# Sums of squares for the norms: additions on VectorE in place of products with ones on TensorE

## The chip, the cores and the metric

One core of one Trainium2 chip runs the whole program in one launch. The metric is the device time of that core in microseconds; the time before is the median of 3 runs. The engines are named as in the profile: PE (TensorE), DVE (VectorE), ACT (ScalarE), POOL (GpSimd), SP (SyncE, which here only issues transfers).

## The reference, cut to what matters

A transformer trunk of two layers works on 256 context tokens and 1024 latent tokens, 1280 in all, with 1024 features in f32. Each layer normalises its tokens, projects them, runs four mixers (mLSTM, latent attention, SSD, S5), projects back, normalises again and runs a feed-forward part of width 2816. The change concerns one function, which occurs with 1024, 256 and 128 features:

```python
def rmsnorm(x, g):
    x32 = x.astype(jnp.float32)
    y = x32 * lax.rsqrt(jnp.mean(x32 * x32, axis=-1, keepdims=True) + EPS)
    return (y * g.astype(jnp.float32)).astype(x.dtype)
```

It is called for both norms of each layer (with a modulation by shift and scale), for the output norm of the SSD mixer, and for the compressed queries, keys and values of the attention. A last norm follows the second layer. (In the kernel, one mixer's per-head norm is computed elsewhere and is not touched.)

## The kernel before, in words

Activations are feature-major: a tile has 128 features on the partitions and tokens along the row. 1024 features are eight tiles. Tokens come in groups of 256 (the context), 512 and 512; layer 1 leaves the context out after its mixers.

A dense product (`dense_acc`, lines 242 to 244) is three matmuls per tile of 128 features, since every f32 operand is split into a leading and a remaining part (`split`, lines 202 and 203). It runs through two PSUM banks, or through five where `many()` is on (the output projection, the feed-forward part, the first products of layer 1).

`rstd` (lines 173 to 197) makes 1/sqrt(mean of squares) for up to 512 tokens, and puts it on every partition. Per tile, ACT squares it (line 181) into a buffer of two, and PE multiplies the squares by a column block of 32 ones (line 183). Tiles go in turn to the four groups of 32 columns of PE's array, so that up to four partial sums lie on four groups of 32 partitions in one PSUM bank. ACT then copies the bank to the tile `sb` (line 186). For each 128 tokens one narrow product (line 188) has 128 columns of `sb` as its stationary operand and a selector column `msel`, with a one on one partition of each group of 32, as its moving operand: it adds up the four partial sums and turns the tokens onto the partitions. DVE scales and adds EPS (line 190), POOL takes the power -0.5 (line 192), PE transposes the broadcast result back (line 194), ACT copies it to SBUF (line 196).

`rstd` is called 30 times:

- at the start, for the three groups (lines 1456 to 1470), eight tiles each; the tile for `sb` has one buffer there, and the squares go to another pool's four buffers;
- in `latent_norms` (line 794), one tile (keys and values) or two (queries) per group, both layers;
- in the SSD outputs (line 650), two tiles per group, both layers, with one buffer that `sb` and the broadcast share;
- in `norm_mod` (line 218) for the second norm of each layer (lines 1623 and 1625), eight tiles per group; `norm_apply` then takes two DVE operations and one ACT operation per tile (lines 212, 214, 215);
- in `done` (lines 1634 to 1646), after the last feed-forward products of a group: in layer 0 the next layer's first norm, in layer 1 the final norm, whose result DVE multiplies in (line 1644) and ACT's queue sends out.

Around the norms of `done` and of lines 1623 and 1625, each dense product of a tile is followed by the residual on DVE, which reads the PSUM bank and updates x (line 1601). x is what line 181 squares.

The order in which the engines work is not that of the text. The program is built with `schedule_with_timeline_sim=True` (line 1829): the builder places the instructions of all engines by a timeline that it simulates, and each engine then takes its own queue in that order. Weight loads on SP's queue are issued within `ahead()`.

## Time and profile before

| what | value |
|---|---|
| median of 3 runs | 3555.32 us (3553.36 to 3558.95) |
| span of the profiled execution, first to last instruction | 3550.2 us |
| mean granted TensorE clock of that execution | 0.981 |
| PE busy, matmuls | 3418.2 us |
| PEld busy, weight loads | 2795.2 us |
| DVE busy | 1708.2 us |
| ACT busy | 1106.9 us |
| POOL busy | 889.9 us |
| products with ones, line 183 | 138 matmuls, 276 records |

The profiled execution's own time is its span, 3550.2 us, and what little lies outside of the first and last instruction; the runs' times are taken without a profile. A matmul of two f32 operands shows as two records. A matmul's start is measured, its end is modelled, and matmuls overlap: distances from start to start tell what one costs in a stream. "idle" in a row is the time in which the engine did nothing just before, with what released it. [...]

### The profile page before, as it was taken

To read this page: it belongs to the slowest core of one execution; us is meant where nothing else is said; L and a number is where in the kernel's file an instruction comes from. 1 tells how busy PE (TensorE), PEld (TensorE's weight loads), DVE (VectorE), ACT (ScalarE), POOL (GpSimd) and SP (SyncE) were. 2 spreads that over 40 slices of the span, in tenths; PEclk is the share of its full clock that TensorE was granted. 3 is DMA by queue.
4 is the path that set the end of the run, shared out by engine and by line. 5 is a ranking of instruction groups with operands and counts; after the bars stand their busy time and mean duration, and the time that the engine had idled before them with its cause. 6 is when DMAs were issued, how large, how long until landed. Compare 5 with 4: busy or idle time off the path is not lost. (4 is left out here: it accounts for less than half of the span.)

```text
span 3550.2 us, 48986 instructions
## 1 busy us (share of the span) xinstructions
PE 3418.2 (96%) x19154; PEld 2795.2 (79%) x19186; DVE 1708.2 (48%) x3597; ACT 1106.9 (31%) x1885; POOL 889.9 (25%) x1061
## 2 busy tenths in 40 slices
PE   8899998999999999999999999998999999999998
PEld 6888995676768888888887889985666688888885
DVE  6857727554365486333323563636633432232333
ACT  4224534334242211111223324533333312212222
POOL 1922424011033222222221011331110223323321
PEclk9899998999999999999999999998999999999999
DMA  5577533345111121111112655542153111111111
GB/s 200 166 205 229 156 119 113 110 140 212 65 46 62 54 90 72 36 36 36 42 40 81 162 166 164 142 150 67 60 204 107 42 42 54 53 42 54 48 46 62
DMA packets 264904, 352.84 MB, mean 99 GB/s; under 512 B 89240, under 2 KB 190304, under 8 KB 264672
## 3 DMA queue, kind: packets, MB, share of 16 engines
q1 hardware_dynamic: 168148, 265.90, 23.5%
q10 hardware_dynamic: 96524, 83.81, 7.5%
q8 instruction: 151, 2.47, 0.3%
q14 instruction: 81, 0.66, 0.1%
HBM read 266.09 MB, written 83.52 MB: 98 GB/s over the span
## 5 line engine op out<-in xcount | busy, mean ns | idle before, releaser
L1601 DVE SCALAR_TENSOR_TENSOR x<-pd,modv,x 128x512 f32<-128x512 f32 (+1 forms) x448 | 299.8, 687 | 233.6 <-PE pd L244 233.2
L242 PE MATMUL pd<-fh,wh_d 128*128 128x512 f32 (+1 forms) x896 | 325.3, 369 | 9.3 <-ACT fh L202 5.7
L242 PE MATMUL ps_g<-hb,wh_g 128*128 128x512 f32 (+1 forms) x880 | 326.0, 370 | 3.2 <-ACT hb L214 2.2
L244 PE MATMUL ps_g<-hb,wl_g 128*128 128x512 f32 (+1 forms) x880 | 324.4, 369 | 2.5 <-POOL wl_g L203 2.5
L243 PE MATMUL pd<-fl,wh_d 128*128 128x512 f32 (+1 forms) x896 | 326.0, 367 | 0.7 <-POOL fl L203 0.7
L244 PE MATMUL pd<-fh,wl_d 128*128 128x512 f32 (+1 forms) x896 | 325.5, 368 | 0.0
L242 PE MATMUL ps_u<-hb,wh_u 128*128 128x512 f32 (+1 forms) x880 | 325.4, 370 | 0.0
L243 PE MATMUL ps_g<-hb,wh_g 128*128 128x512 f32 (+1 forms) x880 | 325.1, 369 | 0.0
L243 PE MATMUL ps_u<-hb,wh_u 128*128 128x512 f32 (+1 forms) x880 | 324.7, 369 | 0.0
L244 PE MATMUL ps_u<-hb,wl_u 128*128 128x512 f32 (+1 forms) x880 | 324.3, 369 | 0.2 <-POOL wl_u L203 0.2
L662 DVE SCALAR_TENSOR_TENSOR cv<-gp,vec,cv 128x1281 f32<-128x1281 f32 (+1 forms) x44 | 72.6, 1651 | 476.8 <-ACT cv L659 476.8
L242 PE MATMUL ps_in<-ha,wh_in 128*128 128x384 f32 (+3 forms) x688 | 218.3, 326 | 13.5 <-ACT st L1426 13.5
L203 POOL TENSOR_TENSOR wl_u<-wr_u,wh_u 128x1024 fp32r<-128x1024 f32 x44 | 105.5, 2397 | 481.7 <-ACT wh_u L202 481.7
L243 PE MATMUL ps_in<-ha,wh_in 128*128 128x384 f32 (+3 forms) x688 | 222.4, 323 | 0.0
L244 PE MATMUL ps_in<-ha,wl_in 128*128 128x384 f32 (+3 forms) x688 | 221.2, 322 | 0.0
L242 PE MATMUL ps_in<-hb,wh_in 128*128 128x256 f32 (+1 forms) x704 | 212.7, 305 | 0.8 <-ACT hb L214 0.6
L244 PE MATMUL ps_in<-hb,wl_in 128*128 128x256 f32 (+1 forms) x704 | 212.8, 303 | 0.0
L243 PE MATMUL ps_in<-hb,wh_in 128*128 128x256 f32 (+1 forms) x704 | 212.5, 302 | 0.2 <-DVE hb L215 0.2
L242 PEld LDWEIGHTS pd<-fh,wh_d 128*128 128x128 f32 x896 | 169.1, 189 | 45.8 <-DVE x L1601 7.4
L202 ACT CAST wh_u<-wr_u 128x1024 fp32r<-128x1024 f32 x44 | 46.3, 1051 | 502.4 <-PE pd L243 436.5
L242 PEld LDWEIGHTS ps_g<-hb,wh_g 128*128 128x128 f32 x880 | 166.2, 189 | 36.4 <-ACT hb L214 3.5
L243 PEld LDWEIGHTS pd<-fl,wh_d 128*128 128x128 f32 x896 | 169.4, 189 | 31.9 <-issue 1.7
(509 smaller groups left out, 7691.2 us busy)
## 6 DMA issues: line engine op xcount, KB each, us to landing
wm<-in_w_mod SPq DMA_DIRECT2D x96, 512.0 KB
wr_in<-in_w_in SPq DMA_DIRECT2D x44, 512.0 KB
wr_g<-in_w_up SPq DMA_DIRECT2D x44, 512.0 KB
wr_u<-in_w_up SPq DMA_DIRECT2D x44, 512.0 KB
wr_d<-in_w_down SPq DMA_DIRECT2D x44, 512.0 KB
wr_out<-in_w_out SPq DMA_DIRECT2D x32, 512.0 KB
PF<-st ACTq DMA_DIRECT2D x100, 128.0 KB
PF<-st ACTq DMA_DIRECT2D x60, 192.0 KB
```

What stands on the lines that cost most here:

```text
L202: nc.scalar.copy(hi, src)
L203: (eng or nc.gpsimd).tensor_tensor(lo, src, hi.bitcast(F32), OP.subtract)
L242: nc.tensor.matmul(ps, whi(k), ahi(k), start=start and i == 0, stop=False)
L243: nc.tensor.matmul(ps, whi(k), alo(k), start=False, stop=False)
L244: nc.tensor.matmul(ps, wlo(k), ahi(k), start=False, stop=stop and i == len(ks) - 1)
L662: nc.vector.scalar_tensor_tensor(dst, src[:, 0:n], w0, dst, OP.mult, OP.add)
L1601: nc.vector.scalar_tensor_tensor(v, ps, K.modv[l][:, 8 * part + m, c:c + 1], v, OP.mult, OP.add)
```

## The change

In `rstd`, ACT squares the first tile straight into `sb`. Each further tile is squared into its buffer as before, and DVE adds it to `sb`. The products with 32 columns of ones and the copy of the bank to `sb` are gone. The PSUM bank is taken after that; the narrow product for each 128 tokens has a column of ones as its moving operand, over all 128 partitions. What follows is as before.

```diff
     def rstd(self, tiles, nfeat, n, pool, name, bufs=2, out=None, sqs=None):
         nc = self.nc
         ntc = n // P
-        ng = min(len(tiles), 4)
-        ps = self.psm.tile([P, 512], F32, tag="m", name=f"ss_{name}")
+
+        sb = pool.tile([P, 512], F32, tag="rb", name=f"sb_{name}", bufs=bufs)
         for i, x in enumerate(tiles):
+            if not i:
+                nc.scalar.activation(sb[:, :n], x, AF.Square)
+                continue
             sq = sqs(f"sq_{name}_{i}") if sqs else pool.tile([P, 512], F32, tag="sq", name=f"sq_{name}_{i}", bufs=bufs)
             nc.scalar.activation(sq[:, :n], x, AF.Square)
-            g = i % 4
-            nc.tensor.matmul(ps[32 * g:32 * g + 32, :n], self.ones[:, :32], sq[:, :n], start=i < 4, stop=i >= len(tiles) - ng)
-        sb = pool.tile([P, 512], F32, tag="rb", name=f"sb_{name}", bufs=bufs)
-        r_ = slice(0, 32 * ng)
-        nc.scalar.copy(sb[r_, :n], ps[r_, :n])
+            nc.vector.tensor_tensor(sb[:, :n], sb[:, :n], sq[:, :n], OP.add)
+        ps = self.psm.tile([P, 512], F32, tag="m", name=f"ss_{name}")
         for j in range(ntc):
-            nc.tensor.matmul(ps[:, j:j + 1], sb[r_, j * P:j * P + P], self.msel[r_, 0:1], start=True, stop=True)
+            nc.tensor.matmul(ps[:, j:j + 1], sb[:, j * P:j * P + P], self.ones[:, 0:1], start=True, stop=True)
         v = pool.tile([P, 8], F32, tag="rs", name=f"rv_{name}", bufs=4)
```

The rest of the diff takes comments out and leaves their lines empty.

## Rows read from the trace of the kernel before

**Rows 1.** The page's first part: busy time (share of the span) xinstructions, by engine.
```profile
PE 3418.2 (96%) x19154; PEld 2795.2 (79%) x19186; DVE 1708.2 (48%) x3597; ACT 1106.9 (31%) x1885; POOL 889.9 (25%) x1061
```

**Rows 2.** Line 183 by stretches: us, PE busy, PEld busy, clock, DMA share, GB/s.
```profile
0.00:40.00 40.00, 11.22 (x48) 3.14 (x48) 0.91 0.88 308
190.00:300.00 110.00, 8.13 (x18) 1.24 (x18) 1.00 0.82 234
400.00:510.00 110.00, 5.42 (x12) 0.82 (x12) 1.00 0.33 95
920.00:1005.00 85.00, 18.19 (x48) 2.64 (x48) 1.00 0.14 47
1905.00:1962.00 57.00, 19.35 (x48) 3.34 (x48) 0.97 0.33 116
2100.00:2160.00 60.00, 6.89 (x14) 0.96 (x14) 1.00 0.44 146
2270.00:2340.00 70.00, 4.18 (x8) 0.55 (x8) 1.00 0.33 95
2690.00:2795.00 105.00, 12.04 (x32) 1.68 (x32) 0.99 0.28 101
3500.00:3540.00 40.00, 15.66 (x48) 3.06 (x48) 0.99 0.11 40
sum 677.00, PE 101.10 PEld 17.43; mean PE 11.23 PEld 1.94
```

**Rows 3.** All instructions by stretches: us, PE, PEld, DVE, ACT, POOL busy, clock, DMA.
```profile
0.00:40.00 40.00, 25.97 (x234) 14.59 (x235) 11.65 (x42) 21.00 (x40) 14.22 (x11) 0.91 0.88 308
190.00:300.00 110.00, 103.77 (x661) 92.83 (x662) 73.22 (x201) 28.74 (x62) 22.07 (x47) 1.00 0.82 234
...
920.00:1005.00 85.00, 85.00 (x363) 55.48 (x363) 29.07 (x48) 29.16 (x50) 9.76 (x9) 1.00 0.14 47
```

**Rows 4.** PE in order of time: start us, us, what; around products of line 183.
```profile
986.97 1.05 PE L183 MATMUL ss_n<-sq_n,ones 128*32 128x512 f32 x4
...
1931.85 0.62 PE L183 MATMUL ss_n<-sq_n,ones 128*32 128x256 f32 x2
...
3502.28 0.39 PE L243 MATMUL pd<-fl,wh_d 128*128 128x512 f32 x1
3502.51 0.40 PE L244 MATMUL pd<-fh,wl_d 128*128 128x512 f32 x1
3502.83 1.04 PE L183 MATMUL ss_fin<-sq_fin,ones 128*32 128x512 f32 x2
3503.81 0.50 PE L242 MATMUL pd<-fh,wh_d 128*128 128x512 f32 x1
```

**Rows 5.** DVE lines: duration ns min/median/max; the last one by form, mean ns.
```profile
L764 DVE TENSOR_TENSOR m_u<-m_u,m_r x18: 681/691/693, 608.2 to 2571.8; 128x512 f32<-128x512 f32 x18
L1154 DVE TENSOR_TENSOR zm_V<-zm_pis,zm_y x32: 408/417/539, 85.6 to 1230.1; 128x256 f32<-128x256 f32 x32
L1601 DVE SCALAR_TENSOR_TENSOR x<-pd,modv,x 128x512 f32<-128x512 f32 x344 | 253.6, 749 | 211.5 <-PE pd L244 211.3
```

**Rows 6.** Three more stretches, columns as in rows 3.
```profile
1908.00:1984.00 76.00, 71.82 (x338) 47.97 (x337) 48.84 (x79) 33.15 (x60) 5.31 (x6) 0.98 0.26 92
2790.00:2800.00 10.00, 5.64 (x23) 2.75 (x20) 2.10 (x4) 3.59 (x6) 1.01 (x1) 0.77 0.01 2
2800.00:2810.00 10.00, 10.00 (x34) 7.79 (x34) 9.12 (x14) 4.27 (x7) 0.00 (x0) 0.72 0.00 0
```

**Rows 7.** PE in order of time, at the start: idle before, and what ended it.
```profile
28.75 0.64 PE L151 MATMUL pm<-wm,sc 128*32 128x128 f32 x16 [2.39 <-DMA wm<-in_w_mod]
```

**Rows 8.** Groups of 3490 to 3550: busy us, mean ns, idle before and releasers.
```profile
L1601 DVE SCALAR_TENSOR_TENSOR x<-pd,modv,x 128x256 f32<-128x256 f32 (+1 forms) x24 | 13.5, 572 | 18.9 <-PE pd L244 18.9
L1644 DVE SCALAR_TENSOR_TENSOR x<-x,vec,rbs_fin 128x256 f32<-128x256 f32 (+1 forms) x24 | 11.9, 569 | 6.4 <-ACT rbs_fin L196 6.4
```

**Rows 9.** Line 181, the squares: duration ns min/median/max, first and last start, forms.
```profile
L181 ACT ACTIVATE sq_n<-x x64: 402/630/636, 878.3 to 2791.3; 128x512 f32<-128x512 f32 x48, 128x256 f32<-128x256 f32 x16
```

## The prediction, made before the change was built

> **What bounds the kernel now.** The page's first part comes first: PE is busy for 96% of the span, DVE for 48% [rows 1]. An average does not say whether PE time that is taken out comes back, so the next view is the products of line 183 alone, stage by stage [rows 2]. They hold PE for 101.1 us, 2.8% of the span, in nine stretches: the start, the latent norms and the SSD norms of both layers, the second norm of both layers (920 and 2690), the norm for layer 1 (1905) and the final norm. Then all engines in those stretches [rows 3]: from 920 to 1005 PE is busy for all of 85 us, in the first 40 us for only 26.0. Line 183 has 138 matmuls and 276 records, two to a matmul.

> What one costs is read from starts, since the ends are modelled [rows 4]. Between dense products of 512 columns the starts are 0.23 us apart. With one 512-column product of line 183 between, they go from 3502.51 to 3503.81, 1.30 us: it costs 1.30 - 0.23 = 1.07 us, close to its record of 1.04. So the busy sums of rows 2 serve as the price. [...]

> **The change part by part.** Durations are those of the profiled execution: its span is 3550.2 us, 5.1 us less than the median of the runs, 3555.3, part of which lies outside the span. I take gains from the span and subtract them from the median.

> *Removed:* the 138 products, 101.1 us of PE, and 30 copies on ACT (line 186), which I cost at nothing in themselves: ACT is not the bound.

> *Added:* one addition per tile but the first. The 14 calls with eight tiles make 7 each, the 10 calls with two tiles one each: 98 + 10 = 108, of which 71 have 512 columns and 37 have 256. The nearest rows are additions or products of two f32 SBUF tiles on DVE: 0.69 us for 512 columns (0.68 to 0.69) and 0.42 for 256 (0.41 to 0.54) [rows 5]. Sum: 71 x 0.691 + 37 x 0.417 = 64.5 us on an engine that has 1842 us free; the dearest 256 would add 4.5.

> *Kept:* the narrow products per 128 tokens, as many as before, with ones in place of the selector. In the small calls they sum over 128 rows instead of 32 or 64; I take no difference, as the output has the same one column.

> *Moved:* the tile sb is taken before the first square, where it was taken after the last product. With two buffers, a group's first square now waits for the narrow products of the group before; at the start and in SSD, with one, for those products or for the last use of the broadcast. Nothing but squares of the same norm is queued behind that on ACT for long, and PE has dense work meanwhile; nothing. The PSUM bank is taken later and held for less; nothing, perhaps a gain. No DMA is added or moved by hand.

> By stages, with the PE time of rows 2:

> - Start, 11.2 us: **0**. PE waits there for the modulation weights, 2.39 us at 28.75 [rows 7], and DVE is idle for 28 of the 40 us [rows 3], enough cover for the 21 additions: 7 x 0.417 + 14 x 0.691 = 12.6 us. If they came late, up to 3 us are lost; without PE work until the weights land, the clock could stay low a little longer: -5 to 0 for both.
> - Latent norms, layer 0, 8.1: **4**, half. PE is busy for 104 of 110 us, but DVE works 73 on the scans beside it, and a chain there may set the end (0 to 8).
> - SSD norms, layer 0, 5.4; latent and SSD norms, layer 1, 6.9 and 4.2: **16.5**, in full. Dense products fill PE there.
> - Second norm, layer 0, 18.2: **18**. PE never idles, and DVE is busy for 29 of 85 us [rows 3].
> - Norm for layer 1, 19.4: **13**. From 1908 to 1984 DVE works 48.8 of 76 us on residuals and on applying the norm [rows 6]; the additions make it 48.8 + 12.6 = 61.4. That leaves 14.6 at most, less about 1.5 of waiting for the first sums. DVE becomes the bound here.
> - Second norm, layer 1, 12.0: **17**. Its last group gets its norm late, since each pair of squares waits for a product in PE's queue. PE is then idle for 4.4 us in 2790 to 2800, and in 2800 to 2810 the granted clock is 0.72, that is, some 5.6 us at 1.2 GHz, which costs 2.8 [rows 6]. With squares and additions off PE's queue the norm is ready while PE still has the first group's products; I count 5 of these 7.2 us (12 to 19).
> - Final norm, 15.7: **9**. DVE waits 18.9 us there for residuals and 6.4 for the broadcast [rows 8]; the additions take 7 x 0.691 + 14 x 0.417 = 10.7. What is left of 25.3 is 14.6, less the wait for the very first residual, about 3, and 2 to 3 for the chain behind the last sum: squares, one narrow product, power, transpose, copy. After the change DVE is late next.

> Sum: 0 + 4 + 16.5 + 18 + 13 + 17 + 9 = 77.5. 3555.3 - 78 = **3477 us**.

> Not shown by the trace: the order of every queue is built anew from a simulated timeline, SP's loads included. What a bad order costs is bounded by the tail of layer 1's second norm, 7 us; four such stages could each gain or lose one, so -28 to +28. I take 0, since nothing says which.

> **The rivals.**

> *A. DVE takes over, and only plain slots come back.* The tails stay as they are and the two stages in which DVE binds give nothing: 16.5 + 18 + 12 + 4 = 50, less 3 at the start: 47, **3508 us**. For it: DVE would be busy for 61 of 76 us around 1908. Against it: DVE is off the path in the other stages.

> *B. The products ran beside each other, so they are cheaper than they look.* At 986.97 two of them (four records) take 1.05 us together, what one takes alone [rows 4]. If a round of up to four always cost 1.07 us at 512 columns and 0.62 at 256 (the record at 1931.85), the 38 rounds after the start would hold PE for 26 x 1.07 + 12 x 0.62 = 35 us, and 3555 - 35 = **3520 us** comes out. Against it: those are rounds that seldom meet. Squares come one or two at a time, and the union of their records is 101 us already.

> [...]

> *C. Slower: the queue of DVE becomes a chain.* DVE works in order. If each addition is queued right behind its residual, DVE stands until ACT has squared that tile, and the next residual, which frees the PSUM bank that PE wants, stands behind it. Then a tile of 512 takes 0.75 (residual) + 0.63 (square) [rows 5, 9] + 0.69 (addition) + some 0.25 of crossings = 2.3 us, where PE needs 6 x 0.23 = 1.37: +0.95. With such gaps the clock falls as it did after the idle time at 2790 [rows 6]; at 1.2 GHz the tile's six products take twice as long, 2.76 us: +1.39. For the 77 additions of the large norms after the start this is 107 us against the 78 gained: 3555 - 78 + 107 = **3584 us**. It decides from 78 / 77 = 1.0 us of stall per addition. Against it: five banks and residuals of other groups are in flight and can be put between, and in the second norms dense products of other groups stand beside the residuals.

> **How the numbers follow.** What a measurement of this kernel can tell from no change is about 0.2%, 7 us. Chances: the forecast 0.61 (its own range 3450 to 3500: start -5, tails +-15, latent 0 to 8, final and layer 1 norms down to half), A 0.19, B 0.08, C 0.08, gains and losses that cancel 0.04. The range reaches from 3450, all slots outside the start (90 us) with both tails and a lucky order, to 3520, which takes in A and just reaches B. Faster: 0.61 + 0.19 + 0.08 = 0.88; same 0.04; slower 0.08.

> **What the changed profile would show.** PE's busy time falls by some 95 us to about 3320, and DVE's rises by some 65 to 1773. No product has 32 columns from line 183. From 920 to 1005 the same dense products take 18 us less. Around 2790 to 2810 PE shows no gap and the clock stays at 1.0. At the end DVE's rows stand nearly back to back. It would be wrong if residuals (line 1601) of a stage are spaced by more than 1.4 us with PE waiting for DVE, if the granted clock falls in the norm stages, or if the 100% stretches gain less than rows 2 give, with new waits of PE for something that is not DVE.

## The result, and the profile after

The changed kernel takes **3489.7 us** (median of 4 runs, 3485.1 to 3493.4), the kernel before 3554.9 in the same comparison: a ratio of 0.9816, 95% interval 0.9803 to 0.983. That is 65 us faster where 78 were forecast, inside the range. The profiled executions say the same: the span goes from 3550.2 to 3483.2 us, 67.0 less.

Busy time by engine, the page's first part, of the changed kernel; it answers to [rows 1]:

```profile
PE 3316.9 (95%) x18910; PEld 2782.9 (80%) x18910; DVE 1758.5 (50%) x3705; ACT 1092.4 (31%) x1853; POOL 893.4 (26%) x1061
```

PE loses 101.3 us: all that line 183 held [rows 2]. DVE gains 50.3. The additions' own records, all of them line 185 in the changed kernel (duration ns min/median/max, first and last start in us, forms):

```profile
L185 DVE TENSOR_TENSOR sb_n<-sb_n,sq_n x77: 415/682/2667, 9.7 to 2727.3; 128x512 f32<-128x512 f32 x56, 128x256 f32<-128x256 f32 x21
L185 DVE TENSOR_TENSOR sb_fin<-sb_fin,sq_fin x21: 410/426/683, 3436.5 to 3472.1; 128x256 f32<-128x256 f32 x14, 128x512 f32<-128x512 f32 x7
L185 DVE TENSOR_TENSOR sb_ln<-sb_ln,sq_ln x5: 426/682/693, 248.1 to 2111.1; 128x512 f32<-128x512 f32 x4, 128x256 f32<-128x256 f32 x1
L185 DVE TENSOR_TENSOR sb_s_r<-sb_s_r,sq_s_r x5: 426/693/827, 413.9 to 2286.7; 128x512 f32<-128x512 f32 x4, 128x256 f32<-128x256 f32 x1
```

There are 108 (77 + 21 + 5 + 5), 71 of 512 columns and 37 of 256, at 0.68 and 0.42 us: as forecast from [rows 5].

All engines in four stretches that the prediction named (us, then busy time of PE, PEld, DVE, ACT, POOL, the granted clock, DMA); the first two answer to [rows 3], the others to the norm for layer 1 in [rows 6], which now comes some 25 to 35 us earlier:

```profile
0.00:40.00 40.00, 17.66 (x167) 13.33 (x168) 22.31 (x67) 17.96 (x34) 14.66 (x11) 0.88 0.88 306
920.00:1005.00 85.00, 80.05 (x379) 65.19 (x378) 53.13 (x91) 36.57 (x55) 18.09 (x14) 0.98 0.14 43
...
1910.00:1920.00 10.00, 2.50 (x12) 2.02 (x11) 9.18 (x18) 5.71 (x10) 0.00 (x0) 0.72 0.58 193
1920.00:1930.00 10.00, 5.56 (x18) 4.56 (x19) 7.08 (x11) 5.74 (x9) 1.01 (x1) 0.50 0.35 122
```

From 920 to 1005 PE had not idled at all; now it idles for 5 us. In the norm for layer 1 it stands for 11.9 of 20 us while DVE is busy for 16.3, and the granted clock falls to 0.5, at which products of 384 columns start 0.32 us apart, not 0.17 as at 1.0 (0.98 over the whole stretch before, [rows 6]). PE's longest wait there, 7.5 us, is that of a narrow product (line 188) for the last addition of its group (line 185). The end of layer 1's second norm looks as forecast; it stood at 2790 to 2810 in [rows 6]:

```profile
2730.00:2740.00 10.00, 7.73 (x38) 6.01 (x38) 3.12 (x6) 3.08 (x5) 3.37 (x2) 1.00 0.16 52
2740.00:2750.00 10.00, 10.00 (x43) 7.66 (x43) 8.09 (x12) 4.32 (x7) 0.00 (x0) 1.00 0.00 0
2750.00:2760.00 10.00, 8.25 (x35) 6.14 (x35) 4.33 (x4) 7.33 (x9) 4.67 (x5) 1.00 0.18 55
```

Gaps of 2.3 and 1.8 us are left, but the clock stays at 1.0.

**Where the 67 us came from.** The same products stand in both programs, so their starts can be set against each other. Six marks cut the program: the first product of the output projection of layer 0 (835.7 us before), the last of `zm_pq` in its feed-forward part (1238.3), the first of layer 1's input projection (1961.1), the last `a_po` of its attention (2686.9), the last `ps_g` (3482.0) and the end (3550.2). The gain between marks, in us of span against the profile of before; the kernels below the changed one are those of the next section. A row is one execution each, so its sum can stand some us from what the medians say (own_tag: 68.9 here, 78 by medians):

| kernel | A: to layer 0's projection | B: second norm, 0 | C: norm for layer 1 | D: latent and SSD norms, 1 | E: second norm, 1 | F: final norm | sum |
|---|---|---|---|---|---|---|---|
| forecast | 9.4 | 18 | 13 | 11.1 | 17 | 9 | 77.5 |
| changed | 9.7 | 15.0 | 10.7 | 10.5 | 17.2 | 3.9 | 67.0 |
| changed_again | 9.9 | 15.2 | 10.6 | 7.8 | 17.9 | 3.8 | 65.2 |
| own_tag | 0.0 | 17.4 | 14.3 | 10.5 | 17.2 | 9.5 | 68.9 |
| own_tag_again | -0.3 | 17.4 | 15.2 | 14.1 | 17.8 | 9.5 | 73.7 |
| no_additions | 12.1 | 18.5 | 23.3 | 11.5 | 15.3 | 17.2 | 97.9 |
| own_tag_no_additions | 10.1 | 27.8 | 22.2 | 16.6 | 20.9 | 17.7 | 115.3 |
| both_ways | 5.4 | -8.4 | -3.2 | -0.7 | -1.0 | -9.8 | -17.7 |
| own_tag_large | 5.7 | 16.6 | 15.2 | 18.7 | 16.8 | 9.5 | 82.5 |
| own_tag_large_ssd | 8.7 | 17.3 | 14.9 | 11.1 | 17.3 | 9.5 | 78.7 |
| large_norms_only | -2.8 | 16.3 | 8.7 | -6.3 | 17.8 | 3.9 | 37.7 |
| own_tag_gpsimd | -16.3 | 8.0 | 12.9 | 13.9 | 16.8 | 9.4 | 44.8 |
| before_own_tag | -7.6 | 0.3 | -0.3 | 1.9 | 0.6 | 1.0 | -4.0 |

A, D and E are as forecast (A by luck, as the runs below show); B and C fall short by 2 to 3, F by 5. F is the clearest. In the changed kernel the last dense product starts at 3453.5 instead of 3526.9, 73 us earlier, but behind it come 29.7 us instead of 23.3. DVE in that tail, in order of time (start, us, what, and in brackets the idle time before it with what ended it):

```profile
3445.25 1.39 DVE L1601 SCALAR_TENSOR_TENSOR x<-pd,modv,x 128x256 f32<-128x256 f32 x3
...
3453.06 5.39 DVE L1644 SCALAR_TENSOR_TENSOR x<-x,vec,rbs_fin 128x512 f32<-128x512 f32 x8 [0.57 <-ACT rbs_fin L196]
3458.37 0.41 DVE L185 TENSOR_TENSOR sb_fin<-sb_fin,sq_fin 128x256 f32<-128x256 f32 x1
3458.70 0.87 DVE L1601 SCALAR_TENSOR_TENSOR x<-pd,modv,x 128x256 f32<-128x256 f32 x2
3459.49 3.06 DVE L185 TENSOR_TENSOR sb_fin<-sb_fin,sq_fin 128x256 f32<-128x256 f32 x6
3463.72 0.16 DVE L190 TENSOR_SCALAR rv_fin<-ss_fin 128x2 f32<-128x2 f32 x1 [1.17 <-PE ss_fin L188]
3465.84 3.25 DVE L1644 SCALAR_TENSOR_TENSOR x<-x,vec,rbs_fin 128x256 f32<-128x256 f32 x8 [1.96 <-ACT rbs_fin L196]
3469.01 3.53 DVE L185 TENSOR_TENSOR sb_fin<-sb_fin,sq_fin 128x256 f32<-128x256 f32 x7
3473.78 0.16 DVE L190 TENSOR_SCALAR rv_fin<-ss_fin 128x2 f32<-128x2 f32 x1 [1.24 <-PE ss_fin L188]
3475.91 3.25 DVE L1644 SCALAR_TENSOR_TENSOR x<-x,vec,rbs_fin 128x256 f32<-128x256 f32 x8 [1.96 <-ACT rbs_fin L196]
```

The residuals of the second group are being made from 3445 on, but its first addition comes at 3458.37, and all seven of the third group stand behind line 1644 of the second. The groups have become a chain. ACT in the same stretch shows what holds them:

```profile
3452.44 0.59 ACT L196 COPY rbs_fin<-ss_fin 128x512 f32<-128x512 f32 x1 [6.65 <-PE ss_fin L194]
3452.92 0.42 ACT L181 ACTIVATE sb_fin<-x 128x256 f32<-128x256 f32 x1
...
3465.43 0.37 ACT L196 COPY rbs_fin<-ss_fin 128x256 f32<-128x256 f32 x1 [2.44 <-PE ss_fin L194]
3465.70 0.42 ACT L181 ACTIVATE sb_fin<-x 128x256 f32<-128x256 f32 x1
```

The first square of a group, the one that goes into `sb`, comes right behind the broadcast copy (line 196) of the group before, although ACT stood idle for 6.65 us and the group's first residual was done. `sb` and the broadcast `rbs` share the tag `rb` with two buffers, which are handed out in turn: sb, rbs, sb, rbs. By this reading the next group's `sb` can be handed out only once the `rbs` of the group before has been; the first run below puts it to the test. Before, `sb` was asked for after all squares of its group, so this held nothing back; now it is asked for ahead of the first.

### The profile page after: what moved, and what is told of

It reads as the page before. It is cut to its first block, busy times and chain, and to the rows that moved or that the text cites. A ratio compares the mean times of both kernels' runs of the same rounds, so it can differ in the third digit from the quotient of the medians.

```text
span 3483.2 us, 48594 instructions
## 1 busy us (share of the span) xinstructions
PE 3316.9 (95%) x18910; PEld 2782.9 (80%) x18910; DVE 1758.5 (50%) x3705; ACT 1092.4 (31%) x1853; POOL 893.4 (26%) x1061
```

## The experiments

Theory 1 was this shared tag. Its rival, theory 2, was that DVE's work is the bound, as the prediction had it for C. Medians are us; ratios are to the kernel before on the same chip, with 95% intervals.

**own_tag.** The two buffers are split, one for each use. In the large and latent norms the SBUF is the same and, as the two buffers were taken in turn, so is what each buffer waits for; only the order of handing out differs. In the SSD norms, where one buffer served both, there are now two.

```diff
-        sb = pool.tile([P, 512], F32, tag="rb", name=f"sb_{name}", bufs=bufs)
+        sb = pool.tile([P, 512], F32, tag="sa", name=f"sb_{name}", bufs=1)
...
-        rb = out if out is not None else pool.tile([P, 512], F32, tag="rb", name=f"rbs_{name}", bufs=bufs)
+        rb = out if out is not None else pool.tile([P, 512], F32, tag="rb", name=f"rbs_{name}", bufs=1)
```

> The changed kernel, with the two buffers that sb and the broadcast take in turn split: one for sb alone, one for the broadcast alone. The same SBUF, the same instructions. Theory 1 (sb is now taken ahead of the first square, so a group's squares and sums are placed behind the broadcast copy of the group before): the first square of a group comes as soon as its first residual is there, the additions fall between the residuals, and the tail behind the last dense product goes from 29.7 us back to 23 or less; the gaps of PE in the norm for layer 1 and the second norm of layer 0 shrink. In all 8 to 16 us less than the changed kernel's 3489.7: 3474 to 3482. Theory 2 (VectorE's own work is the bound in those stages): the additions only change places, less than 4 us.

Measured: 3478.2 (3468.1 to 3483.1), ratio 0.9776 (0.9758 to 0.9794): 11.5 less than the changed kernel, as theory 1 said. The tail behind the last dense product (3457.2 to the end at 3481.2) is 24.0 us, near the 23 or less expected. DVE in it:

```profile
3452.51 0.43 DVE L185 TENSOR_TENSOR sb_fin<-sb_fin,sq_fin 128x256 f32<-128x256 f32 x1 [0.29 <-ACT sb_fin L181]
3452.87 0.48 DVE L1601 SCALAR_TENSOR_TENSOR x<-pd,modv,x 128x256 f32<-128x256 f32 x1
...
3456.75 5.39 DVE L1644 SCALAR_TENSOR_TENSOR x<-x,vec,rbs_fin 128x512 f32<-128x512 f32 x8 [0.16 <-ACT rbs_fin L196]
...
3464.09 1.94 DVE L185 TENSOR_TENSOR sb_fin<-sb_fin,sq_fin 128x256 f32<-128x256 f32 x4 [0.29 <-ACT sb_fin L181]
3465.95 3.25 DVE L1644 SCALAR_TENSOR_TENSOR x<-x,vec,rbs_fin 128x256 f32<-128x256 f32 x8
3469.12 1.48 DVE L185 TENSOR_TENSOR sb_fin<-sb_fin,sq_fin 128x256 f32<-128x256 f32 x3
```

Additions now stand between residuals and ahead of line 1644 of the group before: the third group's start at 3464.09, before its predecessor is scaled. The first square waits for the narrow products alone, which read the one `sb`:

```profile
3452.06 0.42 ACT L181 ACTIVATE sb_fin<-x 128x256 f32<-128x256 f32 x1 [2.57 <-PE ss_fin L188]
```

In the table B gains 2.4 over the changed kernel, C 3.6, F 5.6: 11.6 together. In the repeat of both kernels further down it is 2.2, 4.6 and 5.7, or 12.5. That the medians differ by as much is partly luck: A loses 9.7 in the same profile, which is taken up below, and the two spans are only 2.0 us apart (8.4 in the repeat).

**before_own_tag.** The same two lines in the kernel before.

> The kernel before, with the same split of the two buffers. There sb is taken behind the last square and product of its group, so by theory 1 the shared buffers hold back nothing: no change, within 4 us of 3555. If the split helps here too, by 8 us or more, it is not the move of sb that costs, but the order that the builder happens to find.

Measured: 3554.4, ratio 0.9993 (0.9984 to 1.0002). No change: the shared tag costs only where `sb` is asked for ahead of the squares.

**both_ways.** The old products beside the additions; for the first tile the product reads x.

```diff
+        ng = min(len(tiles), 4)
+        ps = self.psm.tile([P, 512], F32, tag="m", name=f"ss_{name}")
         sb = pool.tile([P, 512], F32, tag="rb", name=f"sb_{name}", bufs=bufs)
         for i, x in enumerate(tiles):
...
+            g = i % 4
+            nc.tensor.matmul(ps[32 * g:32 * g + 32, :n], self.ones[:, :32], sq[:, :n], start=i < 4, stop=i >= len(tiles) - ng)
             nc.vector.tensor_tensor(sb[:, :n], sb[:, :n], sq[:, :n], OP.add)
-        ps = self.psm.tile([P, 512], F32, tag="m", name=f"ss_{name}")
```

> The changed kernel with the old products put back beside the additions: per tile one product with 32 columns of ones into the PSUM bank, which nothing reads (the narrow products overwrite it). If the gain is PE's slots, they come back outside of the start: 90 us by the busy time of the old rows, less what falls into the gaps that PE has now (some 15 to 20 us): 3489.7 + 70 to 90 = 3560 to 3580. If a good part of the gain came from elsewhere (ACT's copies that are gone, shorter chains behind the last square), it stays below 3540.

Measured: 3569.7, ratio 1.0036 (1.0022 to 1.0049): 80 us come back. The products were worth 80 us of time for 101.1 us of busy time (90 outside the start): slots on PE, not ACT's copies, which stay out here. Nothing reads their sum in this run, so it prices the slots and not the chain behind them. It also shows that what the change adds and moves, the shared tag among it, costs some 13 us with the products in place.

**no_additions.** It leaves out the sum over all tiles but the first; the squares are still made. The norms are then those of the first tile alone.

```diff
-            nc.vector.tensor_tensor(sb[:, :n], sb[:, :n], sq[:, :n], OP.add)
```

> The changed kernel without the additions: the squares of all tiles but the first are made and not used, so the norms are those of the first tile alone. sb is still taken ahead of the first square, out of the shared buffers. Theory 1: groups stay behind one another, and in a serial group the squares on ACT (0.42 us for 256 columns, 0.63 for 512) take about as long as the additions (0.41, 0.69), so only 3 to 10 us less: 3480 to 3487, with the tail still over 26 us. Theory 2: VectorE loses its 62 us and its stages are freed: 15 to 25 us less, 3465 to 3475, and the tail falls to some 20 us.

Measured: 3454.9, ratio 0.9712 (0.9696 to 0.9728): 34.8 us less than the changed kernel. Both theories were too low; I had no stage in which the additions could cost that much. DVE's busy time falls by 58 (1758.5 to 1700.3). But the 34.8 us are not the price of that work alone: the narrow products now need the first square only, so a norm no longer waits for its other seven tiles, as the next run shows.

```profile
PE 3318.8 (96%) x18877; PEld 2780.0 (81%) x18910; DVE 1700.3 (49%) x3597; ACT 1093.2 (32%) x1855; POOL 897.6 (26%) x1061
```

**own_tag_no_additions.** Both edits, to see whether these are one price or two.

> The kernel with the buffers split, without the additions (the norms are those of the first tile alone). The additions cost 34.8 us with shared buffers (3489.7 to 3454.9), where I had looked for 3 to 10 (theory 1) or 15 to 25 (theory 2). If the order of the groups and VectorE's work are two separate prices, the split takes another 8 to 12 us off here too: 3443 to 3447. If the shared buffers cost only because the additions stand behind them, the split does nothing here: 3451 to 3458, and the additions cost 20 to 27 us over the 3478.2 of the split alone.

Measured: 3441.3, ratio 0.9681 (0.9665 to 0.9697). The split is worth 13.6 us without additions (3454.9 to 3441.3) and 11.5 with them, but not in the same stages: without them the table has it in B (9.3), E (5.6) and D (5.1), and nothing in C and F, where it helped with them. So two like sums do not make it the same price. Leaving the additions out brings 36.9 with the split (3441.3 to 3478.2) and 34.8 without. By stages, own_tag_again against this kernel, it is 10 in A, 10 in B, 7 in C, 3 in D, 3 in E and 8 in F. In C, DVE is full in the split kernel and PE waits, 4.6 us until ACT has applied the norm (line 214) and 3.6 until GpSimd has taken the power (line 192):

```profile
1910.00:1920.00 10.00, 10.00 (x50) 8.29 (x48) 9.97 (x19) 5.75 (x11) 0.00 (x0) 1.00 0.56 210
1920.00:1930.00 10.00, 1.81 (x8) 1.27 (x7) 10.00 (x21) 7.23 (x13) 1.39 (x1) 0.61 0.76 263
1930.00:1940.00 10.00, 9.84 (x37) 9.29 (x36) 9.86 (x15) 4.71 (x7) 1.59 (x3) 0.54 0.17 52
```

Without the additions, the same stage in this kernel, some 20 to 30 us earlier, lets PE idle for less and leaves the clock alone:

```profile
1890.00:1900.00 10.00, 10.00 (x47) 8.22 (x46) 8.45 (x15) 7.18 (x14) 0.62 (x1) 1.00 0.56 210
1900.00:1910.00 10.00, 8.45 (x50) 7.48 (x49) 9.86 (x16) 5.50 (x8) 1.53 (x3) 1.00 0.65 223
1910.00:1920.00 10.00, 9.57 (x61) 8.93 (x60) 9.61 (x15) 6.06 (x9) 0.00 (x0) 1.00 0.28 93
```

What else is missing shows in the last group of the final norm, PE and DVE of this kernel (its lines are numbered one lower: 187 is the narrow product, 1600 the residual):

```profile
3422.39 0.50 PE L187 MATMUL ss_fin<-ones,sb_fin 128*128 128x1 f32 x4
...
3424.87 0.87 DVE L1600 SCALAR_TENSOR_TENSOR x<-pd,modv,x 128x256 f32<-128x256 f32 x2
```

The narrow products start 2.5 us before the group's last two residuals. In the split kernel they start at 3470.75, behind the last addition, and a norm over all tiles can't do otherwise. So the 35 to 37 us hold two things, the additions' work and the wait for seven tiles, and no run here takes them apart.

**large_norms_only.** The changed kernel, with calls of one or two tiles as before.

```diff
+        if len(tiles) < 8:
+            return self.rstd_old(tiles, nfeat, n, pool, name, bufs, out, sqs)
```

`rstd_old`, not shown, is the function before.

> The changed kernel (shared buffers) with additions in the calls with eight tiles alone; the calls with one or two tiles (latent norms, SSD norms) as before. The prediction gave these calls 20.5 us (4 + 16.5): 3489.7 + 20 = 3510. In the profiles the changed kernel gained 9.7 us by the first output projection of layer 0 and 8.6 in the same stretch of layer 1, 18 in all, but the stretch of layer 0 differs by some 7 us between executions. If only layer 1's part is real: some 3498.

Measured: 3515.8, ratio 0.9891 (0.9876 to 0.9905). The small calls bring 26 us, where 20.5 were forecast. In its profile the difference to the changed kernel is 12.5 in A and 16.8 in D, so both layers have a part, though A moves by as much between programs for other reasons.

**own_tag_gpsimd.** The split kernel with the large norms' additions on GpSimd.

```diff
-            nc.vector.tensor_tensor(sb[:, :n], sb[:, :n], sq[:, :n], OP.add)
+            (nc.gpsimd if len(tiles) == 8 else nc.vector).tensor_tensor(sb[:, :n], sb[:, :n], sq[:, :n], OP.add)
```

> The kernel with the buffers split, the additions of the calls with eight tiles on GpSimd in place of VectorE. If VectorE's time and queue are what the additions cost, and GpSimd (74% idle) can take them: 5 to 20 us less than 3478.2. Against it: an operation of two f32 tiles of 512 columns takes GpSimd 1.30 us where VectorE needs 0.68, seven in a row 9.1, and 2 of the 108 additions of the changed kernel took 2.35 and 2.67 us in place of 0.68, both beside a GpSimd operation of 2.4 us that reads two SBUF tiles and until it ended; then VectorE's SBUF operations stand behind the additions: 10 to 30 us more, 3488 to 3508.

Measured: 3507.4, ratio 0.9867 (0.9852 to 0.9882): 29 us slower than the split kernel, at the upper end of the rival's range. Not all of it is the mechanism that was named: by the marks 16 are lost in A and 9 in B, and A holds large additions only at the very start. In B it can be seen. GpSimd's additions and two VectorE lines of the large norms, by form (busy us, mean ns of one, idle before):

```profile
L185 POOL TENSOR_TENSOR sb_n<-sb_n,sq_n 128x512 f32<-128x512 f32 x56 | 79.7, 1423 | 53.0 <-ACT sq_n L184 35.5 <-issue 9.2 <-ACT sb_n L181 5.4
...
L215 DVE SCALAR_TENSOR_TENSOR hb<-nt,modv,hb 128x256 fp32r<-128x256 f32 x16 | 13.1, 845 | 0.4 <-ACT hb L214 0.4
L212 DVE SCALAR_TENSOR_TENSOR nt<-x,ns,rbs_n 128x256 f32<-128x256 f32 x16 | 11.4, 744 | 5.9 <-ACT rbs_n L196 5.9
```

In the split kernel both VectorE groups have a mean of 480 ns. The unexpected part of this is told at the end.

**own_tag_join.** The split kernel; in the large norms the last square is not added, but taken into the same PSUM sum by a second narrow product.

```diff
-            nc.vector.tensor_tensor(sb[:, :n], sb[:, :n], sq[:, :n], OP.add)
+            if i < 7:
+                nc.vector.tensor_tensor(sb[:, :n], sb[:, :n], sq[:, :n], OP.add)
...
-            nc.tensor.matmul(ps[:, j:j + 1], sb[:, j * P:j * P + P], self.ones[:, 0:1], start=True, stop=True)
+            nc.tensor.matmul(ps[:, j:j + 1], sb[:, j * P:j * P + P], self.ones[:, 0:1], start=True, stop=len(tiles) < 8)
+            if len(tiles) == 8:
+                nc.tensor.matmul(ps[:, j:j + 1], sq[:, j * P:j * P + P], self.ones[:, 0:1], start=False, stop=True)
```

> The kernel with the buffers split; in the calls with eight tiles the last square isn't added: a second narrow product per 128 tokens takes it into the same sum in PSUM. 14 additions fewer on VectorE (8 of 0.68, 6 of 0.41: some 7 us busy) and one addition less in the chain behind a group's last residual; 44 narrow products more on TensorE, some 0.22 us each, 10 us. Where VectorE bounds, it gains, where TensorE does, it loses: within 5 us of 3478.2 either way. If the chain behind the last residual were most of what the additions cost: 8 us or more less.

Measured: 3478.4, ratio 0.9781 (0.9767 to 0.9796): no difference. The last link of the chain is not where most of the 37 us lie; a gain on DVE and a loss on PE of some us each may cancel here.

**changed_again and own_tag_again.** The same two kernels beside each other, to learn whether A's 9.7 and 0.0 were chance.

> The changed kernel once more, beside the split one on the same chip. By the first output projection of layer 0 its profile stood 9.7 us ahead of the kernel before, the split one's 0.0 and that of large_norms_only 2.8 behind. If that is the chance of one execution, this profile stands 0 to 10 us ahead there, and the stages behind it repeat their gains within 2 us: second norm of layer 0 15, norm for layer 1 10.7, second norm of layer 1 17, final norm 3.9. If the orders of the two programs make it: 9.7 again, within 2.

> The split kernel once more, beside the changed one. If the 0.0 us at the first output projection was the chance of one execution: 3 to 12 us ahead of the kernel before this time; if it is the order of this program: 0 again, within 2. Behind it the stages repeat: 17.4, 14.3, 17.2 and 9.5. In the median 8 to 15 us less than the changed kernel in the same rounds.

Measured: 3490.9, ratio 0.9821 (0.9808 to 0.9835), and 3479.7, ratio 0.9791 (0.9778 to 0.9804): 11.2 apart, as before. My guess of chance fell: A repeats to 0.3 us (9.9 and -0.3), so each program has its own value there. B, C, E and F repeat within 1 us, D varies by up to 4.

**own_tag_large and own_tag_large_ssd.** The split in the calls with eight tiles alone (shown), and in those and the SSD norms (where `bufs` is 1).

```diff
+        own = len(tiles) == 8
-        sb = pool.tile([P, 512], F32, tag="rb", name=f"sb_{name}", bufs=bufs)
+        sb = pool.tile([P, 512], F32, tag="sa" if own else "rb", name=f"sb_{name}", bufs=1 if own else bufs)
...
-        rb = out if out is not None else pool.tile([P, 512], F32, tag="rb", name=f"rbs_{name}", bufs=bufs)
+        rb = out if out is not None else pool.tile([P, 512], F32, tag="rb", name=f"rbs_{name}", bufs=1 if own else bufs)
```

> The changed kernel with the buffers split in the calls with eight tiles alone. The last two runs showed that the 0.0 us of the split kernel at the first output projection is no chance (0.3 behind the second time, the changed one 9.9 ahead): there the split costs 10 us, in the latent or SSD norms of layer 0. If so, this kernel stands 9 to 11 us ahead there, has the split's gains in the large norms (second norm of layer 0 2.2, norm for layer 1 4.6, final norm 5.7 over the changed kernel), and comes out 12 us under its 3490: 3474 to 3480. If the loss came with the large norms' split (every queue is ordered anew), 0 again at that mark and some 3485 to 3490.

> The same with the buffers of the SSD norms split too (there sb and the broadcast shared a single buffer); only the latent norms share theirs as in the changed kernel. If the latent norms' split costs the 10 us of layer 0: 9 to 11 us ahead at the first output projection, and up to 6 us more in layer 1's stretch of latent and SSD norms, where the split kernel gained 14.1 and the changed one 7.8: 3470 to 3478. If it is the SSD norms' split: 0 at that mark and 3480 to 3486.

Measured: 3473.5, ratio 0.9775 (0.9755 to 0.9794), and 3474.8, ratio 0.9776 (0.9758 to 0.9793). A stands at 5.7 and 8.7, both under the 9 to 11 that were expected. The second kernel differs from own_tag in the latent norms alone, so in this pair most of the 10 us goes with their split. How it comes to cost them is not shown: every edit orders the queues anew. The two miss none of the large norms' gains, but their ratios can't be told from that of own_tag (0.9776, 0.9791). All split versions beat the kernel before and the changed one, the latter by 9 to 16 us by these ratios.

## Why the prediction was right, and which of its steps were wrong

**The main step held.** The gain is PE's slots. Put back, the products cost 80 us, and rival B, in which they ran beside each other and were worth 35 in all, is out. With the split, B gains 17.4 us for 18.2 of products [rows 2], so the price of [rows 4] is near in a stage that the prediction counted as slots alone. Rival A's mechanism, DVE as the bound, shows in C, but C still gives 10.7 us where A gave it nothing, and the sum was 67, not 47. Rival C's time did not come: in the whole changed kernel DVE stands idle before additions for 15.5 us, most of it until a square is there, where C had 107.

**What makes up the 1.07 us of [rows 4].** They are for the most part not the price of 32 columns. The attention of the kernel before has products of two f32 operands that are 128 columns wide:

```profile
640.63 1.02 PE L939 MATMUL a_po<-a_E,a_vt 128*128 128x512 f32 x2
641.09 0.80 PE L934 MATMUL a_pst<-a_qh,a_kh 97*128 97x512 f32 x1
641.73 0.40 PE L935 MATMUL a_pst<-a_ql,a_kh 96*128 96x512 f32 x1
641.96 0.40 PE L936 MATMUL a_pst<-a_qh,a_kl 96*128 96x512 f32 x1
642.20 1.02 PE L939 MATMUL a_po<-a_E,a_vt 128*128 128x512 f32 x2
```

From one to the next it is 1.57 us, with three products of 0.23 to 0.24 between: some 0.87 is left for the wide one (an estimate from these starts). So most of the 1.07 us is what this product of two unsplit f32 operands costs too, at 128 columns. Some 0.2 is left, and what makes it is not shown.

**The step that failed is "Moved: the tile sb is taken before the first square ... nothing".** I listed what a first square would wait for with two buffers (the narrow products of the group before), and did not see that the buffers are handed out in turn between two uses, so that it is placed behind the broadcast copy (line 196), four steps later. It costs some 12 us in three stages: F (9 forecast, 3.9 measured, 9.5 with the split), C (13, 10.7, 14.3) and B (18, 15.0, 17.4).

**A match that is partly luck.** The split kernel takes 3478 us, the forecast was 3477. Its B, C, E and F agree with the forecast within 2.2 us in both of its profiles. But A gives 0.0 and -0.3 where 9.4 were forecast, and the 9.7 of the changed kernel in A is no better proof: A stood between 12.1 us earlier (no_additions) and 16.3 later (own_tag_gpsimd), and 7.6 later in before_own_tag, whose whole time is that of the kernel before. The prediction had named the order of the queues as unknown, 28 us either way.

**What the additions cost stays open.** The prediction took 95 us from PE's slots and tails (90 outside the start, 5 at layer 1's second norm), and charged 17 for additions that are not hidden (4.1 in layer 0's latent norms, 6.4 in C, 6.7 in F). Without additions and with the split the kernel is 114 us faster, and putting the additions back takes 37 of that away. Both are 20 us more than forecast, as they would be if leaving the additions out also saves some 20 us of waiting for seven tiles. In B that kernel gains 27.8 us where the products held 18.2, in F 17.7 for 15.7, which slots alone can't give. So these runs don't show that either term was mis-sized.

**The signs that were named.** Two signs of being wrong came. The granted clock falls in the norm for layer 1, to 0.5. And from 920 to 1005 PE, busy throughout before, has new waits that are not for DVE: 2.2 us until ACT has applied the norm (line 214), 1.2 until GpSimd has split a weight (line 203); B gains 15.0 instead of 18. The cover that I named for B, "DVE is busy for 29 of 85 us", says nothing of these. At the end of layer 1's second norm the gaps did not vanish, but the clock stays up, and the gain is right in size (17.2 for 17).

**Smaller ones.** The start can't be read by itself, since A holds layer 0's small norms too. In large_norms_only, where they are as before, A is -2.8, inside the -5 to 0 that were given. The first input product is 3.9 us late in the changed kernel's profile, but 3.7 late in before_own_tag too. DVE's busy time rose by 50, not 65: the additions are as long as forecast, but with another operation right behind, the next start comes 0.60 us after that of an addition of 512 columns, not 0.68, as neighbours overlap. The 1.2 GHz of the forecast is a granted clock of 0.50: from 2800.10 to 2805.22 of the kernel before, products of 512 columns start 0.427 us apart, 1.2 columns a ns. At 1.0 they start 0.227 apart, so the time of rival C's six products goes up by a factor of 1.9 there, not 2.

## What to carry to other kernels

When an edit moves the place where a buffer is asked for, follow the whole rotation of its tag: what else takes from it in turn, and when that is asked for. Two uses with different times of life want a tag each, even with no more buffers than before. A run that leaves a step out prices that step together with every wait that hung on it. And an engine at half its time is no cover in itself: price an addition by the stage in which it stands, and by what stands behind it in that engine's queue.

## What was not expected of the hardware

```profile
966.57 2.40 POOL L203 TENSOR_TENSOR wl_d<-wr_d,wh_d 128x1024 fp32r<-128x1024 f32 x1 [4.60 <-ACT wh_d L202]
...
966.86 2.67 DVE L185 TENSOR_TENSOR sb_n<-sb_n,sq_n 128x512 f32<-128x512 f32 x1
```

The addition takes 2.67 us in place of 0.68: it ends at 969.53, 0.56 us behind GpSimd's end at 968.97. Not every one is held: in the changed kernel 14 operations of lines 185, 212 and 215 start while a GpSimd operation of over 1.2 us runs, and 3 are stretched past 1.15 us, all beside a subtraction of line 203. Two more start in the last 0.4 us of such a subtraction. The other nine stand beside powers of at most 32 columns (lines 192, 1000 and 1004), and none of them is held, such as this one:

```profile
26.02 5.84 POOL L1000 TENSOR_TENSOR z_dt<-z_e,z_ldt 128x32 f32<-128x32 f32 x1 [1.73 <-DMA z_ldt<-in_s_ldt]
...
26.67 0.69 DVE L185 TENSOR_TENSOR sb_n<-sb_n,sq_n 128x512 f32<-128x512 f32 x1
```

With the additions on GpSimd, 21 of 28 of lines 212 and 215 are stretched; four of the other seven stand beside powers. Residuals (line 1601), which read one operand from PSUM, start beside such an operation 49 and 69 times in the two kernels; none is stretched (at most 752 ns).

In the changed kernel, then, the three that were held read two SBUF tiles and stood beside a subtraction of 128x1024. The nine beside powers read two as well and were not held: the addition above took 0.69 us in the midst of a power of 5.84 that reads SBUF too. What sets the powers apart is not shown. In the changed kernel the price is small, 2 additions of 108 and some 3.7 us. With the large additions on GpSimd it is larger: the two groups of lines 215 and 212 shown for own_tag_gpsimd have a mean of 845 and 744 ns in place of 480, in a run that is 29 us slower.
